# Adaptive products shared by three engines, and PSUM banks of their own in a fp32 network of mixers and experts

## The chip, the core and the metric

The kernel runs on one core of a Trainium2 chip. The metric is the device time of one execution, in microseconds. A core has TensorE (PE, matrix products into PSUM), VectorE (DVE), ScalarE (ACT), GpSimd (POOL) and SyncE (SP, which here only issues DMA transfers). Each engine has a queue of its own and works through it in order; they meet at semaphores.

## What is computed

All in fp32, for one sequence of 256 tokens of width 1024. A first network of two layers, each a mixer and a convolutional feed-forward stage, then a second block (context, two recurrent mixers, neighbourhood attention, a mixture of experts). The part that matters here is the first network and the vectors that modulate it:

```python
c_act = jax.nn.silu(c)
for l in range(DEPTH):
    mod = (c_act @ ada_w[l] + ada_b[l])[:, None, :]
    sh1, sc1, g1, sh2, sc2, g2 = jnp.split(mod, 6, axis=-1)
    h = _rmsnorm(x, norm_mix_w[l]) * (1 + sc1) + sh1
    x = x + g1 * _mixer(h, ...)
    h = _rmsnorm(x, norm_ffn_w[l]) * (1 + sc2) + sh2
    x = x + g2 * _conv_ffn(h, ffn_w_up[l], ffn_conv_w[l], ffn_conv_b[l], ffn_w_down[l])
```

`c` has batch 1, so `c_act @ ada_w` is a product of a vector with a 1024 x 6144 matrix for each layer; the second block has such a matrix too, used for its context and for its latents. In the mixer, queries and keys come from low-rank latents (`c_q` of 384, `c_kv` of 256, each normed and multiplied by an up-projection), beside them a gated recurrence whose gates are 16 columns of the same input projection:

```python
c_q, c_kv, k_rope, q_m, k_m, v_m, o_m, i_m, f_m, g_mla, g_mlstm = jnp.split(h @ w_in, ...)
q  = _rmsnorm(c_q, q_norm_w) @ w_uq ; kv = _rmsnorm(c_kv, kv_norm_w) @ w_ukv
merged = sigmoid(g_mla) * (y_mla @ w_br_mla) + sigmoid(g_mlstm) * (y_mlstm @ w_br_mlstm)
return merged @ w_out
```

## The kernel before

Activations lie transposed, 128 features on the partitions and 256 tokens along the row. A weight comes from memory in loads of 1 MB (`load`, L442, a tile `raw` of 128x2048; three such buffers, four in the context part at the start), in a fixed order on SP's queue. `split_w` turns each half of 128x1024 into a high part (`hi`, a cast on ACT, L451) and the rest (`lo`, raw - hi on DVE, L453); an activation is split in the same way into `hhi` and `hlo`. One fp32 product is then three matmuls, L474 (high x high), L475 (activation's low) and L476 (weight's low), for each block of 128x128.

PSUM has eight banks, handed out by tag: two `d`, three `a`, two `y`, one `f`. A tile of a tag waits until the tile that had the bank before has been read.

The modulating vectors are computed without PE. `ada` (L524) loads 1 MB, that is two blocks of 128x1024 in which each row belongs to one output, and DVE multiplies each block by the broadcast `c` and sums along the row, in one instruction (L533, `accum_out`). There are 80 such loads: 8 at the start, for the context's own vector, 8 behind the context part, then 64 in the two layers. All but the first 8 are a background generator: `tick()` is called at fixed places of the foreground code and adds a rate to each generator's account; a generator that has a whole step advances by one load. `ADA_PARTS` says which eight columns of the vectors (four loads) belong to which of the four stages, `ADA_RATE` how fast they go; `drain` does what is left at a stage's end.

The foreground in one layer: `mixer` (L660) computes the latents: `latent` squares them on ACT (L684) and scales them by the norm's weight (L685), `normed` forms the reciprocal root and the split `lat`. The third query latent is the first half of a `y` bank (`p2`), and its second half takes the rotated key part and the gates. Then the keys (`keys`, from two `d` banks, read by ACT L718 and DVE L719), the rotated key part (`krm`, a product with `rep`, L731), the values (`pv`, L487 to L489, in two `d` banks), the queries, a convolution, attention and recurrence. The branch projections come last: of each group of four output blocks, two `d` and two `y` banks are merged by the gates (L957 to L959: `mga`, `mgb`) and split into `hhi` and `hlo` for the output projection `wo`. `ffn` (L987) then norms `x`, and alternates up and down products; POOL's only steady work there is `hidl`, the low half of a hidden row (L459, 128x256).

The program's order on each engine is not the order of the code: a scheduler that sees priorities, estimated costs and free buffers sets it, except for the loads.

Of the kernel before, what the change touches and what calls it, by code (L numbers as in the profile page):

```python
# [15 lines left out]
AF = mybir.ActivationFunctionType  # L16
OP = mybir.AluOpType
# [3 lines left out]
T = 256  # L21
# [11 lines left out]
NA_PARTS = {3: (0, "wo2b"), 5: (4, "wo2e"), 7: (6, None)}  # L33
ORDER = ('load',)

ADA_PARTS = (range(2, 6), range(6, 9), range(9, 14), range(14, 18))
ADA_RATE, RK_RATE, MID_RATES = (0.8, 0.45, 0.95, 0.6), 0.8, (0.6, 1.0, 1.0, 1.0, 0.6)

# [311 lines left out]
class Net:  # L352
# [162 lines left out]
    def silu_row(self, c, eng=None):  # L515
# [5 lines left out]
        nc.vector.scalar_tensor_tensor(t, th, 1.0, t, OP.add, OP.mult)  # L521
        return t

    def ada(self, src, c, bias, mod, parts, pool=None):  # L524

        nc = self.nc
        for s in parts:
            for q in range(4 * s, 4 * s + 4):
                raw = self.load(src[q], pool, 3 if pool is None else CX_RAW)
                for r in range(2):  # L530
                    j = 2 * q + r
                    w = raw[:, r * 1024 : r * 1024 + 1024]
                    nc.vector.scalar_tensor_tensor(w, w, 0.5, c, OP.mult, OP.mult, accum_out=mod[:, j : j + 1])  # L533
                yield
            m = slice(8 * s, 8 * s + 8)
            nc.vector.tensor_tensor(mod[:, m], mod[:, m], bias[:, m], OP.add)
# [123 lines left out]
    def mixer(self, l, mp, x, mod):  # L660
        nc = self.nc
        s = str(l)
        mt = lambda shape, name, dt=F32, tag=None: mp.tile([P] + shape, dt, tag=tag or name, name=self.uid(name))
        v2 = lambda ap: ap.rearrange("p (a t) -> p a t", a=2)
        h = self.norm_mod(x, self.V("nmix" + s, 0, 8), mod[:, 8:16], mod[:, 0:8])
# [9 lines left out]
        st = Stream(self, "lat" + s)  # L675
        lat = mt([16, T], "lat", F32R)
        cq, ckv = (tuple(lat[:, o + i * n : o + i * n + n, :] for i in (0, 1)) for o, n in ((0, 3), (6, 2)))
        raw = mt([8, T], "raw", F32, "qf")
# [4 lines left out]
        def latent(j, ps, w):  # L683
            nc.scalar.activation(sqk[:, j, :], ps, AF.Square)  # L684
            nc.scalar.activation(raw[:, j, :], ps, AF.Identity, scale=w)  # L685
# [16 lines left out]
            latent(3 + q, pkv[:, q * T : q * T + T], self.V("kvn" + s, q))  # L702
        for q in range(2):
            latent(q, p01[:, q * T : q * T + T], self.V("qn" + s, q))
        p2 = self.ps("y")
        self.mm3(p2[:, :T], st, h)
        normed(ckv, 3, 2, 256)
        latent(2, p2[:, :T], self.V("qn" + s, 2))
        self.mm3(p2[:, T:], st, h)


        cqp, ckvp = self.parts(cq, range(3)), self.parts(ckv, range(2))
# [1 line left out]
        st = Stream(self, "uq" + s)  # L714

        def keys(b):
            pq = v2(self.proj(st, ckvp))
            nc.scalar.copy(kf[0:64, 4 * b : 4 * b + 4 : 2, :], pq[0:64])  # L718
            nc.vector.tensor_copy(kf[0:64, 4 * b + 1 : 4 * b + 4 : 2, :], pq[64:128])  # L719
# [2 lines left out]
        normed(cq, 0, 3, 384, False)  # L722

        krm = mt([T], "krm")
        nc.vector.tensor_tensor(krm[64:128, :], p2[64:128, T:], self.cs[64:128, :], OP.mult)
        gi, gf = self.tmp(T, "gi", bufs=1, rows=8), self.tmp(T, "gf", bufs=1, rows=8)
        nc.vector.tensor_scalar(gi, p2[0:8, T:], self.V("gb" + s)[0:8], None, OP.add)
        nc.vector.tensor_scalar(gf, p2[32:40, T:], self.V("gb" + s)[32:40], None, OP.add)
        keys(1)
        pk = self.ps("a")  # L730
        nc.tensor.matmul(pk[:, :T], self.C("rep")[64:128, :], krm[64:128, :], start=True, stop=True)  # L731
        nc.scalar.copy(kf[64:128], bcn(pk[64:128, :T], 8))
        pv = [self.ps("d") for _ in range(2)]
        self.mm3n(pv, st, ckvp, 512, False)
        for i in range(2):
            nc.scalar.copy(vn[:, i, :], pv[i])
# [106 lines left out]
        for hd in range(8):  # L843
# [10 lines left out]
            for i, c in enumerate((slice(0, P), slice(P, 3 * P))):  # L854
                nc.scalar.activation(e[:, c], ps[:, c], AF.Exp, bias=mx[:, i : i + 1], scale=(64 + 32) ** -0.5,
                                     accum_out=msum[:, i, hd : hd + 1])
# [89 lines left out]
        st = Stream(self, "br" + s)  # L946
        fl = lambda ap: ap.rearrange("p a t -> p (a t)")
        for j0 in (0, 4):
            pas, pbs = ([self.ps(t) for _ in range(2)] for t in "dy")
            for ps, yp in ((pas, yap), (pbs, ymp)):  # L950
                for q in range(4):
                    self.mm3(ps[q // 2][:, q % 2 * T : q % 2 * T + T], st, yp)
                    if q % 2 and ps is pbs:
                        j = j0 + q - 1
                        pa, pb = pas[q // 2], pbs[q // 2]
                        ta, tb = self.tmp(512, "mga"), self.tmp(512, "mgb")
                        nc.vector.scalar_tensor_tensor(ta, fl(sg[:, j : j + 2, :]), 1.0, pa, OP.add, OP.mult)  # L957
                        nc.vector.scalar_tensor_tensor(tb, fl(sg[:, 8 + j : 10 + j, :]), 1.0, pb, OP.add, OP.mult)
                        nc.vector.tensor_tensor(ta, ta, tb, OP.add)  # L959
                        self.split(m[0][:, j : j + 2, :], m[1][:, j : j + 2, :], v2(ta))  # L960
                        self.tick()
        gh = self.np.tile([P, 8], F32, tag="gh", name=self.uid("gh"))
        nc.vector.tensor_scalar(gh, mod[:, 16:24], 0.5, None, OP.mult)
        st = Stream(self, "wo" + s)
        mp_ = self.parts(m, range(8))
        for i in range(4):
            ps = self.proj(st, mp_)
            for c in range(2):
                j = 2 * i + c
# [17 lines left out]
    def ffn(self, l, fp, x, mod, rk):  # L987
# [14 lines left out]
        self.background(rk, RK_RATE)  # L1002
        self.background(self.ada_of(ADA_PARTS[2 * l + 1]), ADA_RATE[2 * l + 1])
        for op in _ffn_order():
# [77 lines left out]
    def first(self):  # L1082
        nc, x = self.nc, self.x
        with self.pool("cxm") as cxp, self.pool("cb") as self.cbp:
            with self.pool("rope") as rp:
# [7 lines left out]
                for l in range(2):  # L1093
                    self.part = 1
                    self.background(self.ada_of(ADA_PARTS[2 * l]), ADA_RATE[2 * l])
                    with self.pool(f"mix{l}") as mp, self.phase(f"m{l}", {256: 6, 384: 5, 512: 5}):
# [1072 lines left out]
```

## Time and profile before

| | us |
|---|---|
| runs: median of 3 (lowest to highest) | 1775.16 (1772.66 to 1775.33) |
| the profiled execution, its own time | 1772.79 |
| its span, first to last instruction | 1770.9 |
| mean granted clock of TensorE, share of full speed | 0.946 |
| busy: PE / DVE / ACT / POOL | 1579.1 / 1128.0 / 758.6 / 77.9 |

By the trace the context part runs to about 128 us, the first mixer to 310, its feed-forward stage to 550, the second mixer to 765, its feed-forward stage to 1003, the second block's mixers to 1314, and the experts to the end. A row of a timeline reads: start, duration, engine, line, operation, output tile <- input tiles, shape, and in brackets how long the engine was idle before it and what it waited for. A row of waits reads: who waited for whom, us in total, times, longest. Matmuls overlap: a row shows 0.28 us where one follows the other about every 0.12 us. The names of tiles are those of the code; where a line belongs to a helper (L442, L451, L453, L458, L459, L474 to L476), the tile tells what it is.

### The profile page before, as it was taken

The page shows a single profiled execution, that of the slowest core. Times are in us where ns is not written, and L with a number is a line of the kernel's source. Part 1 is how long each engine was busy: PE and PEld are TensorE (multiplying, and loading weights), DVE is VectorE, ACT ScalarE, POOL GpSimd, SP SyncE. Part 2 cuts the span into 40 slices and gives each one's busy share as a digit, 9 for nine tenths or more (in the row PEclk, how much of TensorE's full clock was granted, in tenths as well). Part 3 has the DMA queues.
Part 4 walks back from the last instruction along what each step waited for, and adds up shares of the span by engine and source line. Part 5 has one row for each costly group of instructions (what it writes and reads, how often), then busy time and mean ns, then how long its engine had stood idle before and what let it go on. Part 6 is the DMA issues. An engine that isn't in the chain of part 4 may idle for free.

```text
span 1770.9 us, 32054 instructions
## 1 busy us (share of the span) xinstructions
PE 1579.1 (89%) x13278; PEld 1269.7 (72%) x13278; DVE 1128.0 (64%) x2167; ACT 758.6 (43%) x1256; POOL 77.9 (4%) x81
## 2 busy tenths in 40 slices
PE   3989999999998999989999999999989877776766
PEld 2988999899998899979999999878874312221211
DVE  7979878798887898879989778766662111011011
ACT  3566545664455654556454576464431100000000
POOL 0000000020010000001010101000000000000000
PEclk7999999999999999999999999998989889888888
DMA  9745675556674478565667543123369999999998
GB/s 392 312 142 191 242 281 204 209 207 221 217 250 143 169 266 319 216 237 179 239 228 289 194 171 114 67 98 134 144 249 403 419 417 416 417 416 419 419 417 340
DMA packets 76808, 460.78 MB, mean 260 GB/s; under 512 B 8563, under 2 KB 11123, under 8 KB 28147
## 3 DMA queue, kind: packets, MB, share of 16 engines
q1 hardware_dynamic: 74352, 452.45, 67.0%
q10 hardware_dynamic: 2306, 6.24, 1.0%
q8 instruction: 106, 1.74, 0.4%
q14 instruction: 44, 0.35, 0.1%
HBM read 457.61 MB, written 1.05 MB: 259 GB/s over the span
## 4 chain that ended last, share of the span: by engine, by line
PE 63%; DMA 23%; DVE 8%; ACT 4%; issue 2%; POOL 0%; SPq 0%; DVEq 0%; ACTq 0%; POOLq 0%
DMA ew<-in_wgu 11%; PE d L474 10%; PE d L476 10%; PE d L475 10%; DMA ew<-in_wdown 8%; PE y L474 4%; PE y L476 3%; PE y L475 3%; PE a L1392 3%; DVE lo L453 2%; PE d L2052 2%; DVE raw L533 2%; PE a L1981 1%; PE a L628 1%; DMA raw<-in_ws 1%
## 5 line engine op out<-in xcount | busy, mean ns | idle before, releaser
L451 ACT CAST hi<-raw 128x1024 fp32r<-128x1024 f32 x309 | 322.4, 1048 | 303.2 <-PE d L475 186.2
L453 DVE TENSOR_TENSOR lo<-raw,hi 128x1024 fp32r<-128x1024 f32 x309 | 379.1, 1233 | 90.3 <-ACT hi L451 88.5
L474 PE MATMUL d<-hhi,hi 128*128 128x256 f32 x1320 | 387.9, 295 | 29.4 <-ACT hhi L591 23.7
L475 PE MATMUL d<-hlo,hi 128*128 128x256 f32 x1320 | 381.3, 289 | 3.2 <-DVE hlo L594 1.7
L476 PE MATMUL d<-hhi,lo 128*128 128x256 f32 x1320 | 380.2, 288 | 0.2 <-DVE lo L453 0.2
L474 PEld LDWEIGHTS d<-hhi,hi 128*128 128x128 f32 x1320 | 258.4, 196 | 38.3 <-ACT hhi L591 26.3
L475 PEld LDWEIGHTS d<-hlo,hi 128*128 128x128 f32 x1320 | 259.3, 196 | 6.6 <-DVE hlo L594 2.9
L476 PEld LDWEIGHTS d<-hhi,lo 128*128 128x128 f32 x1320 | 259.0, 196 | 1.4 <-DVE lo L453 0.4
L2052 PE MATMUL d<-ew,xe 128*32 128x512 f32 x984 | 165.3, 704 | 56.5 <-DMA ew<-in_wgu 56.0
L533 DVE SCALAR_TENSOR_TENSOR raw<-raw,cb 128x1024 f32<-128x1024 f32 x160 | 193.9, 1228 | 5.4 <-DMA raw<-in_ada 5.0
L2052 PEld LDWEIGHTS d<-ew,xe 128*32 128x32 f32 x984 | 26.1, 116 | 170.5 <-DMA ew<-in_wgu 145.7
L2057 DVE SCALAR_TENSOR_TENSOR moa<-moa,d 128x512 f32<-128x512 f32 x8 | 5.5, 687 | 178.4 <-ACT moa L2056 178.4
L474 PE MATMUL y<-hhi,hi 128*128 128x256 f32 x352 | 100.8, 286 | 4.6 <-ACT raw L685 3.9
L476 PE MATMUL y<-hhi,lo 128*128 128x256 f32 x352 | 100.0, 285 | 0.9 <-DVE lo L453 0.9
L475 PE MATMUL y<-hlo,hi 128*128 128x256 f32 x352 | 99.6, 283 | 0.0
L2070 PE MATMUL y<-ew,mht 128*32 128x512 f32 x472 | 74.4, 687 | 26.6 <-DMA ew<-in_wdown 22.4
L2088 DVE SCALAR_TENSOR_TENSOR x<-f,mod_l,x 128x256 f32<-128x256 f32 x32 | 14.0, 479 | 127.8 <-PE f L2084 127.8
L459 POOL TENSOR_TENSOR hidl<-fgel,hidh 128x256 fp32r<-128x256 f32 x44 | 54.2, 1233 | 838.4 <-ACT hidh L458 817.3
L2056 ACT ACTIVATE moa<-d 128x512 f32<-128x512 f32 x8 | 4.8, 597 | 184.7 <-PE d L2052 184.7
L474 PEld LDWEIGHTS y<-hhi,hi 128*128 128x128 f32 x352 | 67.4, 192 | 6.1 <-ACT raw L685 4.7
L2070 PEld LDWEIGHTS y<-ew,mht 128*32 128x32 f32 x472 | 13.0, 117 | 78.3 <-DMA ew<-in_wdown 58.6
L476 PEld LDWEIGHTS y<-hhi,lo 128*128 128x128 f32 x352 | 67.4, 192 | 1.4 <-DVE lo L453 1.1
(676 smaller groups left out, 3193.7 us busy)
## 6 DMA issues: line engine op xcount, KB each, us to landing
raw<-in_ws SPq DMA_DIRECT2D x151, 1024.0 KB, 4.8
ew<-in_wgu SPq DMA_DIRECT2D x100, 1024.0 KB, 18.0
raw<-in_ada SPq DMA_DIRECT2D x80, 1024.0 KB, 4.9
ew<-in_wdown SPq DMA_DIRECT2D x46, 1024.0 KB, 19.7
ew<-in_wgu SPq DMA_DIRECT2D x46, 512.0 KB, 13.8
ew<-in_wdown SPq DMA_DIRECT2D x28, 512.0 KB, 12.5
two<-in_wgu SPq DMA_DIRECT2D x20, 256.0 KB, 8.4
two<-in_wdown SPq DMA_DIRECT2D x16, 256.0 KB, 8.1
```

Source lines behind the costliest of these rows:

```text
L451: f.append(nc.scalar.copy(hi_, raw))
L453: f.append(nc.vector.tensor_tensor(lo_, raw, hi_.bitcast(F32), OP.subtract))
L459: (eng or self.nc.vector).tensor_tensor(lo, src, hi.bitcast(F32), OP.subtract)
L474: nc.tensor.matmul(out, whi, hhi, start=first and i == 0, stop=False, **s)
L475: nc.tensor.matmul(out, whi, hlo, start=False, stop=False, **s)
L476: nc.tensor.matmul(out, wlo, hhi, start=False, stop=last and i == n - 1, **s)
L533: nc.vector.scalar_tensor_tensor(w, w, 0.5, c, OP.mult, OP.mult, accum_out=mod[:, j : j + 1])
L628: self.nc.tensor.transpose(out, in_, self.C("ident")[:k, :k])
L1392: nc.tensor.matmul(ps[r, g * 64 : g * 64 + 64], l_(g, p, r), r_(g, p, r), start=True, stop=True, skip_group_check=True)
L1981: nc.tensor.matmul(ps[:, k * P : k * P + P], xn[:, i, d : d + P], of(i), start=i == 0, stop=i == 1, skip_group_check=True)
L2052: nc.tensor.matmul(ps[32 * e : 32 * e + 32, :], xe[:, k, 32 * e : 32 * e + 32], w[e], start=k == 0, stop=k == 7, skip_group_check=True)
L2070: nc.tensor.matmul(py[q][32 * e : 32 * e + 32, :], ht[:, f * P + 32 * e : f * P + 32 * e + 32], w[e], start=f == 0, stop=f == 3, skip_grou ...
```

## The change

Three things, and two tables of numbers. First, the two blocks of each adaptive load are no longer treated alike: the first is multiplied by POOL in place and then halved and summed along its row by ACT; the second stays on DVE. 80 of the 160 products of DVE become 80 of POOL and 80 of ACT. Second, the `tick()` after each of the four merges of the branch projections is gone; four loads (one range of `ADA_PARTS`) go from the second mixer's stage to the first feed-forward stage, and two rates are lower. Third, the third query latent and the gates have a `y` bank each (`p2`, `pg`), and the values take two `y` banks where they took two `d` banks.

```diff
-ADA_PARTS = (range(2, 6), range(6, 9), range(9, 14), range(14, 18))
-ADA_RATE, RK_RATE, MID_RATES = (0.8, 0.45, 0.95, 0.6), 0.8, (0.6, 1.0, 1.0, 1.0, 0.6)
+ADA_PARTS = (range(2, 6), range(6, 10), range(10, 14), range(14, 18))
+ADA_RATE, RK_RATE, MID_RATES = (0.8, 0.45, 0.8, 0.45), 0.8, (0.6, 1.0, 1.0, 1.0, 0.6)
...
+    def ada_block(self, w, c, out, shared):
+
+        nc = self.nc
+        if shared:
+            nc.gpsimd.tensor_tensor(w, w, c, OP.mult)
+            nc.scalar.activation(w, w, AF.Copy, scale=0.5, accum_out=out)
+        else:
+            nc.vector.scalar_tensor_tensor(w, w, 0.5, c, OP.mult, OP.mult, accum_out=out)
+
...
                 for r in range(2):
-                    j = 2 * q + r
-                    w = raw[:, r * 1024 : r * 1024 + 1024]
-                    nc.vector.scalar_tensor_tensor(w, w, 0.5, c, OP.mult, OP.mult, accum_out=mod[:, j : j + 1])
+                    self.ada_block(raw[:, r * 1024 : r * 1024 + 1024], c, mod[:, 2 * q + r : 2 * q + r + 1], r == 0)
                 yield
...
-        p2 = self.ps("y")
-        self.mm3(p2[:, :T], st, h)
+        p2, pg = (self.ps("y")[:, :T] for _ in range(2))
+        self.mm3(p2, st, h)
         normed(ckv, 3, 2, 256)
-        latent(2, p2[:, :T], self.V("qn" + s, 2))
-        self.mm3(p2[:, T:], st, h)
+        latent(2, p2, self.V("qn" + s, 2))
+        self.mm3(pg, st, h)
...
-        pv = [self.ps("d") for _ in range(2)]
+        pv = [self.ps("y") for _ in range(2)]
         self.mm3n(pv, st, ckvp, 512, False)
...
                         self.split(m[0][:, j : j + 2, :], m[1][:, j : j + 2, :], v2(ta))
-                        self.tick()
```

The order of the instructions moves at three places. The numbers behind a tile's name are the program's own and differ between the two kernels; lines after the new function are six or seven higher.

ACT near 41 to 55 us, in the context part; `x` (here `two_120..123<-x_74`, its four squares) has been loaded by then, `cpad` is the context's first projection, copied out of a `d` bank that PE needs again. Before:

```order
L451 CAST hi_37_281<-raw_36_279 128x1024
L451 CAST hi_39_309<-raw_36_279 128x1024
L451 CAST hi_44_350<-raw_43_348 128x1024
L561 ACTIVATE two_120_987<-x_74 128x512
L561 ACTIVATE two_121_989<-x_74 128x512
L561 ACTIVATE two_122_992<-x_74 128x512
L561 ACTIVATE two_123_997<-x_74 128x512
L451 CAST hi_46_378<-raw_43_348 128x1024
L541 ACT_TABLE_LOAD
L1216 COPY cpad0_222<-d_32_225 128x2x256
L1216 COPY cpad1_223<-d_33_226 128x2x256
```

Now:

```order
L451 CAST hi_37_289<-raw_36_287 128x1024
L451 CAST hi_39_317<-raw_36_287 128x1024
L529 ACTIVATE raw_41_351,mod0_75<-raw_41_351 128x1024
L451 CAST hi_44_359<-raw_43_357 128x1024
L529 ACTIVATE raw_48_418,mod0_75<-raw_48_418 128x1024
L451 CAST hi_46_387<-raw_43_357 128x1024
L568 ACTIVATE two_120_1003<-x_74 128x512
L568 ACTIVATE two_121_1005<-x_74 128x512
L1222 COPY cpad0_230<-d_32_233 128x2x256
L568 ACTIVATE two_122_1008<-x_74 128x512
L1222 COPY cpad1_231<-d_33_234 128x2x256
```

Two halves of adaptive blocks stand among the casts, and the first copy stands behind two squares where it stood behind four and a table load.

PE where the keys end and the values begin, layer 0 (`d_156`, `d_164` before and `d_157`, `d_165` now are the two banks of keys, `a_` the rotated key part, `d_166` before and `y_167` now the first bank of values). Before:

```order
L475 MATMUL d_164_1277<-lat_131_1039,hi_158_1244 128x256
L476 MATMUL d_164_1277<-lat_131_1039,lo_159_1245 128x256
L731 MATMUL a_165_1292<-krm_161_1271,kon_31_220 128x256
L487 MATMUL d_166_1295<-hi_168_1297,lat_131_1039 128x512
L488 MATMUL d_166_1295<-lo_169_1298,lat_131_1039 128x512
L489 MATMUL d_166_1295<-hi_168_1297,lat_131_1039 128x512
```

Now:

```order
L476 MATMUL y_148_1186<-hhi_125_1021,lo_154_1229 128x256
L699 MATMUL f_134_1058<-sqk_133_1057,ones_68 128x256
L474 MATMUL d_157_1258<-lat_131_1055,hi_159_1261 128x256
L474 MATMUL d_165_1294<-lat_131_1055,hi_159_1261 128x256
L738 MATMUL a_166_1309<-krm_162_1288,kon_31_228 128x256
L487 MATMUL y_167_1312<-hi_169_1314,lat_131_1055 128x512
L475 MATMUL d_157_1258<-lat_131_1055,hi_159_1261 128x256
L476 MATMUL d_157_1258<-lat_131_1055,lo_160_1262 128x256
```

The first matmul of each key bank, the rotated part and the first matmul of the values now come right behind the gates (`y_148`), before the rest of the keys.

ACT where the branch projections of layer 0 end and `wo` begins (`hhi_416` before and `hhi_417` now are the merged rows' high halves; the last of the four opens the last blocks of `wo`). Before:

```order
L451 CAST hi_462_3234<-raw_459_3204 128x1024
L458 CAST hhi_416_2919<-mga_450_3155 128x512
L451 CAST hi_466_3268<-raw_465_3266 128x1024
L458 CAST hhi_416_2919<-mga_455_3194 128x512
L382 DMA kon_482_3459<-in_k_rk 128x1216
```

Now:

```order
L451 CAST hi_458_3224<-raw_457_3222 128x1024
L529 ACTIVATE raw_462_3282,mod0_75<-raw_462_3282 128x1024
L451 CAST hi_460_3252<-raw_457_3222 128x1024
L458 CAST hhi_417_2949<-mga_449_3177 128x512
L451 CAST hi_465_3290<-raw_464_3288 128x1024
L529 ACTIVATE raw_469_3348,mod0_75<-raw_469_3348 128x1024
L458 CAST hhi_417_2949<-mga_453_3212 128x512
```

Two adaptive halves stand here, one of them just ahead of the last merged row's cast.

## Rows read from the trace of the kernel before

**Rows 1.** busy us (share of the span) of each engine, part 1 of the page

```profile
PE 1579.1 (89%) x13278; PEld 1269.7 (72%) x13278; DVE 1128.0 (64%) x2167; ACT 758.6 (43%) x1256; POOL 77.9 (4%) x81
```

**Rows 2.** busy time by stretches of the span; the first row names the columns

```profile
core 0: us, PE busy (x) PEld busy (x) DVE busy (x) ACT busy (x) POOL busy (x), PEclk, DMA share, GB/s
177.00:232.00 55.00, 52.83 (x429) 50.06 (x429) 48.63 (x89) 30.45 (x68) 0.00 (x0) 1.00 0.68 250
298.00:310.00 12.00, 12.00 (x103) 12.00 (x103) 11.86 (x18) 5.63 (x7) 0.00 (x0) 1.00 0.77 277
340.00:550.00 210.00, 208.39 (x2092) 202.46 (x2091) 181.67 (x313) 113.00 (x178) 27.45 (x22) 0.99 0.61 219
1314.00:1771.00 457.00, 344.23 (x2016) 113.78 (x2016) 63.98 (x173) 39.40 (x82) 0.38 (x1) 0.86 0.98 402
```

**Rows 3.** waits of PE, 340 to 550 us: us in total, times, longest us

```profile
PE y L475 <- POOL hidl L459: 1.4, 2, 1.0
```

**Rows 4.** costliest groups, part 5: busy us, mean ns of one | idle before

```profile
L451 ACT CAST hi<-raw 128x1024 fp32r<-128x1024 f32 x309 | 322.4, 1048 | 303.2 <-PE d L475 186.2
L453 DVE TENSOR_TENSOR lo<-raw,hi 128x1024 fp32r<-128x1024 f32 x309 | 379.1, 1233 | 90.3 <-ACT hi L451 88.5
...
L533 DVE SCALAR_TENSOR_TENSOR raw<-raw,cb 128x1024 f32<-128x1024 f32 x160 | 193.9, 1228 | 5.4 <-DMA raw<-in_ada 5.0
...
L459 POOL TENSOR_TENSOR hidl<-fgel,hidh 128x256 fp32r<-128x256 f32 x44 | 54.2, 1233 | 838.4 <-ACT hidh L458 817.3
```

**Rows 5.** single lines: times, duration in ns min/median/max, first and last start

```profile
L459 POOL TENSOR_TENSOR hidl<-fgel,hidh x44: 726/1298/1825, 360.5 to 1008.3; 128x256 fp32r<-128x256 f32 x44
...
L1728 POOL TENSOR_TENSOR two<-two,kon x8: 994/999/1108, 1183.3 to 1283.4; 128x384 f32<-128x384 f32 x8
...
L855 ACT ACTIVATION_READ_ACCUMULATOR esm<-a,mx x32: 192/197/206, 160.3 to 666.0; 128x1 f32 x32
```

**Rows 6.** timeline, 364 to 368 us: start us, us, engine, line, operation, tiles

```profile
364.51 2.90 DVE L453 TENSOR_TENSOR lo<-raw,hi 128x1024 fp32r<-128x1024 f32 x2
...
364.71 1.61 POOL L459 TENSOR_TENSOR hidl<-fgel,hidh 128x256 fp32r<-128x256 f32 x1 [2.68 <-ACT hidh L458]
```

**Rows 7.** timeline of the start, DVE and ACT, and a wait of PE

```profile
16.27 1.22 DVE L533 SCALAR_TENSOR_TENSOR raw<-raw,cb 128x1024 f32<-128x1024 f32 x1 [3.20 <-DMA raw<-in_ada]
...
18.75 1.22 DVE L533 SCALAR_TENSOR_TENSOR raw<-raw,cb 128x1024 f32<-128x1024 f32 x1
...
27.29 2.36 DVE L453 TENSOR_TENSOR lo<-raw,hi 128x1024 fp32r<-128x1024 f32 x2 [1.19 <-ACT hi L451]
...
36.87 0.43 ACTq L1183 DMA_DIRECT2D x<-in_xT  x1
...
48.99 2.20 ACT L561 ACTIVATE two<-x 128x512 f32<-128x512 f32 x4 [1.51 <-DMA x<-in_xT]
...
53.44 1.08 ACT L1216 COPY cpad<-d 128x512 f32<-128x512 f32 x2
...
PE d L474 <- ACT cpad L1216: 1.9, 1, 1.9
```

**Rows 8.** timeline of the latents, keys and values, layer 0

```profile
134.47 0.38 PE L474 MATMUL y<-hhi,hi 128*128 128x256 f32 x1 [1.92 <-ACT raw L685]
...
135.84 0.69 DVE L459 TENSOR_TENSOR lat<-raw,lat 128x512 fp32r<-128x512 f32 x1 [0.35 <-ACT lat L458]
...
143.17 0.94 DVE L459 TENSOR_TENSOR lat<-raw,lat 128x768 fp32r<-128x768 f32 x1
...
144.77 0.50 PE L487 MATMUL d<-hi,lat 128*128 128x512 f32 x1 [1.67 <-DVE kf L719]
```

**Rows 9.** waits of PE in the branch projections, layer 0, 284 to 298 us

```profile
PE d L474 <- ACT hi L451: 1.7, 2, 1.2
PE d L476 <- DVE lo L453: 0.2, 1, 0.2
```

**Rows 10.** timeline of DVE at the start of the output projection, layer 0

```profile
313.07 0.69 DVE L459 TENSOR_TENSOR hlo<-mga,hhi 128x512 fp32r<-128x512 f32 x1 [0.69 <-ACT hhi L458]
```

More of the change, by code (lines that the diff above doesn't have):

```diff
@@ L724, in mixer @@
         krm = mt([T], "krm")
-        nc.vector.tensor_tensor(krm[64:128, :], p2[64:128, T:], self.cs[64:128, :], OP.mult)
+        nc.vector.tensor_tensor(krm[64:128, :], pg[64:128], self.cs[64:128, :], OP.mult)
         gi, gf = self.tmp(T, "gi", bufs=1, rows=8), self.tmp(T, "gf", bufs=1, rows=8)
-        nc.vector.tensor_scalar(gi, p2[0:8, T:], self.V("gb" + s)[0:8], None, OP.add)
-        nc.vector.tensor_scalar(gf, p2[32:40, T:], self.V("gb" + s)[32:40], None, OP.add)
+        nc.vector.tensor_scalar(gi, pg[0:8], self.V("gb" + s)[0:8], None, OP.add)
+        nc.vector.tensor_scalar(gf, pg[32:40], self.V("gb" + s)[32:40], None, OP.add)
         keys(1)
```

## The prediction

> **What bounds the kernel now.** I read the busy table first, then the stages, then waits inside a stage. TensorE (PE) is busy 89% of the span, VectorE (DVE) 64%, ScalarE (ACT) 43%, GpSimd (POOL) 4% [rows 1]. By stretches [rows 2] the end of the program is another matter: from 1314 us on the DMA engines are busy 0.98 of the time and PE works on what they bring; no adaptive product and no mixer lies there, so what the change wins or loses before 1003 us is carried through as it is. In the stages that it touches, PE is busy 92 to 99% and hardly waits: in the 210 us of the first feed-forward stage its listed waits are 1.4 us [rows 3]. DVE, at 48.63 of 55 us in the attention [rows 2], is the next limit. So 105 us of DVE work taken away (80 products of 1.23 and an accumulator read of 0.08 us) is no 105 us of time: in most places PE has nothing to get back.
>
> **Price of a shared product.** Before, each 128x1024 block costs DVE 1.228 us, 160 in all [rows 4], and the read of the accumulator. The change sends 80 of them through POOL and ACT. No row shows POOL at 128x1024. Its 128x256 product takes 726 ns at best and its 128x384 one 994 ns [rows 5]: 268 ns for 128 more elements, so 726 + 768 x 2.09 = 2.33 us is my estimate. ACT then reads the block back: its pass over 128x1024 is 1.048 us [rows 4], and the accumulator read beside its exponentials is 0.197 us [rows 5], so 1.25 us. A block thus turns from 1.31 us of one engine into 3.6 us on two in a row.
>
> **POOL and DVE do not run side by side.** POOL's 128x256 product has a median of 1.298 us against 0.726 us at best [rows 5]. At 364.71 us it takes 1.61 us while two DVE differences with both inputs in SBUF, 2 x 1.22 us elsewhere, take 2.90 us around it [rows 6]: 0.88 us longer for POOL, some 0.5 us longer for DVE. One waits for the other. The Trainium skill has a rule against this change, "SBUF — State Buffer", section "Who interferes with whom": the port pair that POOL shares with DVE is locked for a whole instruction, and a DVE instruction with two SBUF inputs contends with a POOL instruction that reads SBUF; the stretched pair of rows agrees, and by the rule the sum is the forecast, without it the first rival.
>
> So I charge DVE for a held lock. It is in operations with two SBUF inputs most of the time (the casts' differences and the products alone are 573 of its 1128 us [rows 1, 4]); it runs into a 2.33 us hold somewhere between not at all and wholly. I take the middle, 1.2 us, because the differences come in pairs right behind the casts, and because POOL's hold is three times that of the row in which DVE lost 0.5. Saved 1.31, lost 1.2: DVE gains about nothing per block (bounds: it gains 1.31, or loses 1.02).
>
> **Start (0 to 58 us), 8 shared blocks.** Here DVE is a chain: products at the pace at which the loads land (16.27, 18.75: 2.48 us apart), two differences, four products, then the gain, h, and behind h's high half in ACT's queue the load of x at 36.87, which has landed 12.1 us later; the four squares of x start at 48.99, cpad at 53.44, and PE waits for cpad [rows 7]. A load would take 2.33 + 1.22 = 3.55 us where it took 2.45 with both blocks on DVE. Four loads lag by 4.4 us, DVE's idle 1.19 us before the differences [rows 7] absorbs a part, and the last two loads add 2.2: mod_c comes 5.4 us later, x lands near 54.3. ACT's new order gives back: cpad0 stands behind two squares and no table load, 1.1 us after x and not 4.45. So cpad at 55.4: +2.0, and with the two products of ACT in the same queue I take **+2.5** (bounds -1.5, were the lock nothing, and +6.5). The 8 blocks of the context's background: **+1** (0 to +3, at 0.4 us each).
>
> **Latents and values in their own banks.** The gate product waited 1.92 us for ACT to read the latents out of the same bank, and the values 1.67 us for DVE to empty a d bank [rows 8]; both waits have lost their cause, once in each of the two layers. The second goes whole, since in the new order the first value product is far ahead of its rest and the query latents, 143.17 + 0.94 = 144.1, are in time. Of the first, what is late next is the low half of the key latents, ready at 135.84 + 0.69 = 136.5 [rows 8]; the gate product used to end near 137.4, so 0.9 is left. Two layers: 2 x 2.6 = **-5.1** (bounds -7.2 and -2).
>
> **No tick beside the branch projections.** PE loses 1.7 us there to a cast and 0.2 to a difference, layer 1 alike [rows 9]: the weight loads stood in the 3 raw buffers behind adaptive ones, and DVE had products between the merges. Two layers: **-3.8** (bounds -5 and 0). But the steps that left are now at the branch's end and in the output projection: one load's ACT product stands just before the last hhi, whose difference DVE waited for at 313.07 already [rows 10], and its POOL product has to be over first. PE has the first seven blocks of the projection to cover it, 21 products of 0.117 us (103 in 12 us, [rows 2]) = 2.5 us, against 2.33 + 0.5 + 1.25 = 4.1 us of POOL and ACT behind the landing. I take **+2.5** for both layers together (0 to +6).
>
> **Attention** (13 shared blocks in each layer): DVE stays as full as it was, and ACT, whose exponentials and casts PE works on next, gets 13 x 1.25 = 16 us more. Between nothing and 0.4 us per block, 0 to 5 us; I take 2 per layer, **+4**. **Norms before the feed-forward stages**: one POOL product lands among the sixteen two-input operations by which h is made: between 0 and 2.3 a layer, **+1.5**. **Feed-forward**: 32 shared blocks; PE's waits of 1.4 us show the cover, and ACT has 113 of 210 us in use [rows 2]. The first stage also takes four loads from the second mixer. **+2** (-2 to +8).
>
> Sum: 2.5 + 1 - 5.1 - 3.8 + 2.5 + 4 + 1.5 + 2 = +4.6 us. The profiled execution took 1772.79 us (span 1770.9), 2.4 below the median of 1775.16; so 1777.4 for it, and **1780** against the median. A difference of 0.2%, 3.5 us, is about what a measurement of this kernel can tell from no change.
>
> **Rivals.** (A) *The lock hardly costs DVE anything*: POOL slips between, starts as soon as a load lands (its queue is nearly empty in these stages), and DVE keeps its 1.31 us per block. Then the start costs nothing (2.33 us per load is under the landing pace of 2.48), norms and feed-forward nothing, attention wins about 2 where PE waits for DVE. For it: the shortest POOL products show no wait at all [rows 5], and DVE is idle a third of the span [rows 1]. Against: the median of 1.298. It gives -5.1 - 3.8 - 2 = -10.9: 1764. (B) *ACT waits in its queue for POOL*, on the slow side: in the new order ACT's half stands about eight PE products, 1 us, behind POOL's, which needs 2.33 + 0.5 with the mean wait of the page (1.233 - 0.726); so ACT stalls some 1.8 us each time with casts behind it, whose differences wait behind them on DVE, and PE behind both. If 0.35 us of that comes through for each of the 72 blocks after the start: 25 - 8.9 + 3.5 = +20: 1795. It decides from about 0.2 us a block. For it: DVE already waits 88.5 us for casts [rows 4]. Against: PE's cover in the feed-forward stages, and loads that often land before their turn. (C) *The banks and ticks do not give what they say*: what stands next is just as late, and sharing is neutral: 1775.
>
> **How the numbers follow.** The forecast 0.47 (faster 0.03, same 0.15, slower 0.29); A 0.30, all faster; B 0.16, all slower; C 0.07 (0.01, 0.05, 0.01). Faster 0.34, same 0.20, slower 0.46. Alone, the forecast runs from 1773 to 1787. The range takes in A at 1764 and B at 1795 and a little beyond: 1763 to 1797.
>
> **What would show it.** POOL's product near 2.3 us at its least and near 2.9 at its median; DVE differences and products of 2 us and over beside it, so that DVE's busy time falls by far less than 105 us (under A it falls by about 100). cpad near 55.4 and PE's first long row after it 2 us later. No wait of PE at the gate product beyond 1 us, none at the values, none for casts in the branch. The forecast is wrong if the span to 1003 us shrinks (A), or if PE's waits for casts in the feed-forward stages come to over 10 us (B); it is also wrong in its steps if the mixer keeps its length while the start does not grow.

## The result and the profile after

The changed kernel takes 1847.97 us (median of 4 runs, 1842.55 to 1860.35) against 1774.13 us: a ratio of 1.0426, 95% interval 1.0373 to 1.0479, **74 us slower**. The side was the one forecast, the size was not: 1780 had been given and 1797 was the end of the range.

The profiled execution of the changed kernel took 1860.35 us, the slowest of the four, 12 us above their median, so its trace shows a loss of 88 us where the runs say 74. Its busy times and costliest groups (parts 1 and 5 of the page; us in total, mean ns of one, then the idle time before):

```profile
PE 1606.2 (86%) x13278; PEld 1292.9 (70%) x13278; DVE 1161.7 (63%) x2013; ACT 831.3 (45%) x1408; POOL 302.1 (16%) x161
...
L453 DVE TENSOR_TENSOR lo<-raw,hi 128x1024 fp32r<-128x1024 f32 x309 | 421.0, 1369 | 101.3 <-ACT hi L451 99.7
...
L528 POOL TENSOR_TENSOR raw<-raw,cb 128x1024 f32<-128x1024 f32 x80 | 227.6, 2849 | 604.9 <-DMA raw<-in_ada 346.7
...
L529 ACT ACTIVATE raw<-raw 128x1024 f32<-128x1024 f32 x80 | 84.8, 1060 | 164.1 <-POOL raw L528 163.8
L531 DVE SCALAR_TENSOR_TENSOR raw<-raw,cb 128x1024 f32<-128x1024 f32 x80 | 128.8, 1613 | 36.4 <-DMA raw<-in_ada 36.1
```

Against [rows 1] and [rows 4]: DVE does 80 instructions fewer that took 1.31 us each, and is busy 34 us longer. The differences that stayed on it went from 1233 to 1369 ns each, its 80 remaining products from 1228 to 1613 ns. ACT stood 163.8 us before its halves, waiting for POOL. The shortest, median and longest of POOL's product, by its line:

```profile
L528 POOL TENSOR_TENSOR raw<-raw,cb x80: 2328/2684/3467, 12.8 to 1084.3; 128x1024 f32<-128x1024 f32 x80
```

The stages (busy us of each engine, then the granted clock, DMA share, GB/s): attention of layer 0, and the two feed-forward stages.

```profile
core 0: us, PE busy (x) PEld busy (x) DVE busy (x) ACT busy (x) POOL busy (x), PEclk, DMA share, GB/s
195.00:255.00 60.00, 53.25 (x408) 50.51 (x408) 45.63 (x73) 34.18 (x71) 17.39 (x6) 0.94 0.64 228
356.00:605.00 249.00, 225.99 (x2158) 216.59 (x2157) 208.92 (x321) 137.90 (x224) 70.44 (x38) 0.96 0.57 208
868.00:1106.00 238.00, 220.65 (x2125) 213.31 (x2124) 197.56 (x313) 127.28 (x204) 69.96 (x37) 0.95 0.60 216
```

PE used to be busy 208.39 of 210 us in such a stage at a granted clock of 0.99 [rows 2]; now it is 226 of 249 at 0.96. The matmuls are the same 13278; at half clock each of them is busy for longer (step 4 below).

Where the time came from is read by the casts of the weights' halves (L451): there are 309 in each kernel, in the same order, so the start of the same cast tells how far a kernel has come. The third column is a kernel of the experiments, the changed kernel with all products on DVE; its distance to the changed kernel is what the sharing cost in each stretch. These are single executions: that of the changed kernel is 12 us above the median of its runs, that with all on DVE 9.

| stretch, from cast to cast | changed - before, us | all on DVE - before | sharing costs | its terms in the prediction |
|---|---|---|---|---|
| start and context (to 24) | +11.4 | -0.2 | 11.6 | 3.5 |
| mixer 0 (to 72) | +10.4 | -4.3 | 14.7 | 3.2 |
| feed-forward 0 (to 144) | +30.5 | +4.4 | 26.0 | 1.8 |
| mixer 1 (to 198) | +8.8 | -6.8 | 15.5 | 3.2 |
| feed-forward 1 (to 270) | +25.9 | -1.1 | 27.0 | 1.8 |
| behind them (to 288) | 0.0 | +1.5 | -1.4 | 0 |
| sum | +87.0 | -6.5 | 93.4 | 13.5 |

More than half of the cost, 53 of 93 us, lies in the two stages that the prediction held to be covered. The other parts of the change do gain what was forecast of them.

### The profile page after: what moved, and what is told of

It reads as the page before. It is cut to its first block, busy times and chain, and to the rows that moved or that the text cites. A ratio compares the mean times of both kernels' runs of the same rounds, so it can differ in the third digit from the quotient of the medians.

```text
span 1858.5 us, 32319 instructions
## 1 busy us (share of the span) xinstructions
PE 1606.2 (86%) x13278; PEld 1292.9 (70%) x13278; DVE 1161.7 (63%) x2013; ACT 831.3 (45%) x1408; POOL 302.1 (16%) x161
## 5 line engine op out<-in xcount | busy, mean ns | idle before, releaser
L453 DVE TENSOR_TENSOR lo<-raw,hi 128x1024 fp32r<-128x1024 f32 x309 | 421.0, 1369 | 101.3 <-ACT hi L451 99.7
L451 ACT CAST hi<-raw 128x1024 fp32r<-128x1024 f32 x309 | 321.0, 1046 | 204.8 <-PE d L475 125.0
L476 PE MATMUL d<-hhi,lo 128*128 128x256 f32 x1320 | 384.5, 292 | 5.8 <-DVE lo L453 5.7
L528 POOL TENSOR_TENSOR raw<-raw,cb 128x1024 f32<-128x1024 f32 x80 | 227.6, 2849 | 604.9 <-DMA raw<-in_ada 346.7
L529 ACT ACTIVATE raw<-raw 128x1024 f32<-128x1024 f32 x80 | 84.8, 1060 | 164.1 <-POOL raw L528 163.8
L531 DVE SCALAR_TENSOR_TENSOR raw<-raw,cb 128x1024 f32<-128x1024 f32 x80 | 128.8, 1613 | 36.4 <-DMA raw<-in_ada 36.1
L2076 PE MATMUL y<-ew,mht 128*32 128x512 f32 x472 | 69.8, 654 | 28.3 <-DMA ew<-in_wdown 24.2
```

Of the source, the lines that this page charges most:

```text
L451: f.append(nc.scalar.copy(hi_, raw))
L453: f.append(nc.vector.tensor_tensor(lo_, raw, hi_.bitcast(F32), OP.subtract))
L476: nc.tensor.matmul(out, wlo, hhi, start=False, stop=last and i == n - 1, **s)
L528: nc.gpsimd.tensor_tensor(w, w, c, OP.mult)
L529: nc.scalar.activation(w, w, AF.Copy, scale=0.5, accum_out=out)
L2076: nc.tensor.matmul(py[q][32 * e : 32 * e + 32, :], ht[:, f * P + 32 * e : f * P + 32 * e + 32], w[e], start=f == 0, stop=f == 3, skip_grou ...
```

## Experiments

Two theories stood at the start. Theory 1: POOL's product, reading SBUF, keeps DVE out, and PE runs out of rows behind DVE. Theory 2: ACT, whose half stands soon behind POOL's in its queue, waits for POOL with casts behind it. A third came out of the runs: POOL holds the load's buffer longer, so that the next load is issued late. A ratio is that of a kernel to the kernel before measured on the same chip; 1% is 17.7 us. The experiments ran on several chips, so what one costs over another is taken from their ratios and not from their medians. Where POOL's product is left out or comes too late, the vectors are wrong; apart from one kernel, told below, PE still does the same 13278 matmuls, and the times can be compared.

**All 160 products on DVE** (the other parts of the change stay).

```diff
-self.ada_block(raw[...], c, mod[...], r == 0)
+self.ada_block(raw[...], c, mod[...], False)
```

> The changed kernel with all 160 products on DVE again; the PSUM banks, the tables and the missing ticks of the branch stay. Both theories (DVE shut out by POOL's reads; ACT's queue held up by POOL) say the whole loss of 74 us goes, and what is left is the gain of the other parts: 1774 - 5.1 - 3.8 = 1765 us. If the tables or the moved steps cost something by themselves, 1774 or more.

Measured: 1762.03 us, ratio 0.9942 (0.9918 to 0.9966), 10 us faster than before. So the sharing alone carries the loss: 0.9942 to 1.0426 is 4.84%, 86 us, 1.07 us for each of the 80 blocks.

**The sharing alone**, put into the kernel before.

> The kernel before with the sharing alone (80 products to POOL and ACT; old banks, ticks and tables). Both theories: slower than the changed kernel by what its other parts gain, 1848 + 9 = 1857 us. If the other parts interact badly with the sharing (the rates crowd the feed-forward stage), below 1840.

Measured: 1858.13 us, ratio 1.0502 (1.0458 to 1.0547). The sharing costs 89 us without the other parts and 86 with them: within the uncertainty (about 0.5% each) the parts add up, and the tables of rates have no visible share in the loss.

**POOL only writes** the block, twice, and ACT waits for that as before.

```diff
-            nc.gpsimd.tensor_tensor(w, w, c, OP.mult)
+            for _ in range(2): nc.gpsimd.memset(w, 0.0)
```

> The changed kernel with POOL filling the block twice with zeros in place of the product: about 2 us of POOL per block that reads nothing, and ACT waits for it as before. The product itself is left out, so the vectors are wrong by half. Theory 1 (POOL's read shuts DVE out): DVE's differences and products go back to 1.23 us and the time to 1780 us or below. Theory 2 (ACT stands in its queue until POOL is done): most of the loss stays, 1830 us or more, with ACT waiting over 100 us for POOL.

Measured: 5699.56 us, which is no comparison: with these vectors the experts get more work (PE does 27278 matmuls and not 13278), and the last part takes over 4 ms. Up to the experts the trace can be compared: cast 288 starts at 1065.5 us, 12 us earlier than before and 5.5 earlier than with all on DVE, one execution of each. POOL's fills, the differences of DVE and ACT's wait (groups by line, then a row of the waits):

```profile
L528 POOL MEMSET raw<- 128x1024 f32 x160 | 152.6, 954 | 575.6 <-DMA raw<-in_ada 346.6 <-DVE lo L453 108.3 <-issue 72.3
```

```profile
L453 DVE TENSOR_TENSOR lo<-raw,hi 128x1024 fp32r<-128x1024 f32 x309 | 376.6, 1222 | 125.2 <-ACT hi L451 121.8
```

```profile
ACT raw L529 <- POOL raw L528: 52.7, 40, 3.5
```

POOL works 1.9 us on each block right in front of ACT, DVE's differences are at 1222 ns, and nothing is lost. This is against theory 2 as the main cause, and it agrees with the rule of the Trainium skill named in the prediction ("SBUF — State Buffer", "Who interferes with whom"), in its other half: a POOL instruction that only writes SBUF does not contend with a DVE instruction of two inputs.

**ACT first, POOL afterwards.** Nobody waits for POOL's result.

```diff
-            nc.gpsimd.tensor_tensor(w, w, c, OP.mult)
             nc.scalar.activation(w, w, AF.Copy, scale=0.5, accum_out=out)
+            nc.gpsimd.tensor_tensor(w, w, c, OP.mult)
```

> The changed kernel with the two halves of a shared block swapped: ACT sums the unmultiplied block as soon as it is there, POOL multiplies it afterwards and nobody reads its result, so the vectors are wrong. DVE is shut out as before, ACT waits for nothing of POOL. Theory 1: 1835 us or more, DVE's operations as long as in the changed kernel. Theory 2: 1785 us or below.

Measured: 1834.96 us, ratio 1.0365 (1.0327 to 1.0403). ACT's wait for POOL is gone and 0.61% is won, 11 us with an uncertainty of about as much (the two intervals together give 0.65%). Theory 2 is at most a small part; the rest stays, and DVE's operations are longer than ever. Its busy times (part 1), then its two groups on DVE:

```profile
PE 1594.9 (87%) x13278; PEld 1284.2 (70%) x13278; DVE 1176.3 (64%) x2019; ACT 831.0 (45%) x1402; POOL 299.2 (16%) x161
```

```profile
L453 DVE TENSOR_TENSOR lo<-raw,hi 128x1024 fp32r<-128x1024 f32 x309 | 434.3, 1412 | 77.4 <-ACT hi L451 75.8
L531 DVE SCALAR_TENSOR_TENSOR raw<-raw,cb 128x1024 f32<-128x1024 f32 x80 | 129.8, 1625 | 38.5 <-DMA raw<-in_ada 38.3
```

**The same without POOL's product.**

> The kernel e4 (ACT's half first, nobody waits for POOL) without POOL's product: 80 blocks are summed by ACT unmultiplied, and POOL does nothing for them. The vectors come out as in e4, wrong in the same way. Theory 1 (POOL's read shuts DVE out): DVE has 105 us less to do and nobody blocks it: 1750 to 1762 us, some 75 us below e4. If ACT's own load were the cost: within 20 us of e4.

Measured: 1750.05 us, ratio 0.9895 (0.9860 to 0.9931). The same vectors as in the kernel just told, the same work on ACT; only POOL's product is missing, and 4.70% with it, **83 us**.

```profile
PE 1573.8 (90%) x13278; PEld 1265.9 (73%) x13278; DVE 1043.1 (60%) x2017; ACT 831.5 (48%) x1404; POOL 77.0 (4%) x81
```

```profile
L453 DVE TENSOR_TENSOR lo<-raw,hi 128x1024 fp32r<-128x1024 f32 x309 | 376.9, 1224 | 134.7 <-ACT hi L451 132.2
L531 DVE SCALAR_TENSOR_TENSOR raw<-raw,cb 128x1024 f32<-128x1024 f32 x80 | 97.4, 1219 | 17.9 <-DMA raw<-in_ada 17.6
```

DVE is busy 133 us less: that is what POOL's 80 products took from it, 1.66 us each. PE's listed waits, summed over the first 1160 us, fall from 117.5 to 57.6 us; those for the weights' low halves, which DVE forms, with the product and without:

```profile
PE d L476 <- DVE lo L453: 14.1, 8, 2.8
```

```profile
PE d L476 <- DVE lo L453: 0.5, 2, 0.2
```

This is theory 1. The kernel also shows how little there was to win: with 80 products off DVE and nothing on POOL in their place it is only 0.47% faster than with all on DVE, 8 us with an uncertainty of as much.

**Half as many shared blocks**, every other load.

```diff
-self.ada_block(raw[...], c, mod[...], r == 0)
+self.ada_block(raw[...], c, mod[...], r == 0 and q % 2 == 0)
```

> The changed kernel with 40 of the 160 products shared in place of 80 (every other load). If each shared block costs the same wherever it lies: half of the way from 1762 to 1848, 1805 us. If the cost comes from crowding (two POOL products close together, ACT's queue filling up), nearer to 1785.

Measured: 1802.54 us, ratio 1.0170 (1.0126 to 1.0213): 2.28% above all-on-DVE for 40 blocks, 1.01 us each, where 80 cost 1.07 each. The cost goes with the number; crowding has no visible share.

**Shared in the feed-forward stages alone** (`r == 0 and self.part == 2`).

> The changed kernel with the sharing in the two feed-forward stages alone (32 products; the 48 others on DVE). By the prediction these stages hide nearly all of it: 1762 + 2 = 1764 us. By the cost per block that the half-shared kernel showed (1.0 us a block anywhere): 1762 + 32 = 1794 us; by the changed kernel's trace, in which the two stages alone grew by some 45 us: 1805 us.

Measured: 1804.88 us, ratio 1.0155 (1.0107 to 1.0203): 2.13%, 38 us for 32 blocks, 1.2 us each, give or take 0.3. The stages that were to hide the blocks pay about as much for one as the others, or more.

**The banks alone, and the ticks with the tables alone** (the kernel before with only that part).

> The kernel before with the PSUM banks alone (p2 and pg in two y banks, the values in y). By the prediction's term: -5.1 us, so 1768.5 against 1773.5. If the next wait is just as late: no change.

> The kernel before without the ticks beside the branch projections and with the new tables, nothing shared. By the prediction's term: -3.8 us at the branch, a little given back where the output projection starts: 1770 to 1772. If what moved costs as much where it now stands: no change.

Measured: ratio 0.9992 (0.9967 to 1.0016) and 0.9980 (0.9958 to 1.0003). Both intervals take in the expected gain (-0.3%, -0.2%) and also no change: undecided one by one. Together, in the kernel with all on DVE, they are 0.9942.

**POOL's product in four pieces**, as the changed kernel waits for it, and with ACT first.

```diff
-            nc.gpsimd.tensor_tensor(w, w, c, OP.mult)
+            for k in range(0, 1024, 256): nc.gpsimd.tensor_tensor(w[:, k : k + 256], w[:, k : k + 256], c[:, k : k + 256], OP.mult)
```

> The changed kernel with POOL's product cut into four of 128x256, so that DVE can get in after 0.73 us and not after 2.33; POOL works 4 x 0.73 = 2.9 us on a block. If the length of one hold is what hurts (DVE stands for a whole instruction, PE runs out of rows): 1815 us or below. If the sum of the holds counts (DVE loses what POOL takes): 1848 us or above.

> The kernel e4 (ACT's half first, nobody waits for POOL, vectors wrong as there) with POOL's product in four pieces of 128x256. It tells apart the two readings of the kernel with four pieces, in which DVE's operations were hardly longer and ACT waited 282 us for POOL. If its 1937 us came from ACT's queue waiting for a product four times interrupted: well below e4's 1835, about 1790, since DVE loses less to a short hold. If DVE's loss to POOL counts however it is cut: 1835 us or above.

Measured: 1936.58 us, ratio 1.0928 (1.0891 to 1.0966), and 1871.40 us, ratio 1.0535 (1.0502 to 1.0568). Both times lie where the second reading had put them, but not for its reason. Shorter holds do spare DVE: its differences are down to 1263 ns from 1369, and it is busy 67 us less than in the changed kernel; yet the kernel is 89 us slower. With ACT waiting, the rows of the first are these (busy times; DVE's differences; ACT's wait):

```profile
PE 1631.2 (85%) x13278; PEld 1312.4 (68%) x13278; DVE 1094.9 (57%) x2013; ACT 827.2 (43%) x1408; POOL 417.8 (22%) x401
```

```profile
L453 DVE TENSOR_TENSOR lo<-raw,hi 128x1024 fp32r<-128x1024 f32 x309 | 388.4, 1263 | 163.7 <-ACT hi L451 161.9 <-PE a L635 0.7
```

```profile
ACT raw L529 <- POOL raw L528: 281.8, 63, 9.6
```

ACT's wait rises from 164 to 282 us: the product is done later, four pieces of 1.115 us in the mean where one took 2.849. Swapping the halves takes 70 us of it away (1.0928 to 1.0535), so here theory 2 is real. What is left is still 30 us above the uncut product with ACT first, and there the waits for loads have grown (ACT and DVE for their blocks of an adaptive load):

```profile
ACT raw L528 <- DMA raw<-in_ada: 131.5, 57, 7.8
DVE raw L531 <- DMA raw<-in_ada: 108.5, 48, 6.7
```

With one product ACT's was 60.2 us and DVE's 38.3. That agrees with the third theory, of a buffer that POOL holds longer.

**A product that belongs to nothing.** ACT sums as in the kernel without a product; POOL then multiplies columns of `c` by themselves into a tile of its own, holding no load. (`spare` is a tile of 128x944 in bf16; its first column is copied from ACT's sum, so that the product starts behind it.)

```diff
+            nc.gpsimd.tensor_copy(self.spare[:, :1], out)
+            nc.gpsimd.tensor_tensor(self.spare, c[:, :944], c[:, :944], OP.mult)
```

> The kernel e5 (ACT sums the unmultiplied block, vectors wrong as there) with a product on POOL that belongs to nothing: after each of ACT's 80 sums POOL multiplies 944 columns of the broadcast c by themselves into a tile of its own. It holds no buffer of a load and nobody waits for its result, so what is left of e4 is POOL's reading beside DVE. If DVE's loss to POOL's reads is the cause: 944/1024 of the way from 1750 to 1835, 1820 us or more. If it was the load's buffer, held until POOL is done: 1765 us or below.

Measured: 1805.23 us, ratio 1.0175 (1.0156 to 1.0193), 2.80% or 50 us above the kernel without it, between the two readings. Its busy times, and the spare product:

```profile
PE 1589.6 (88%) x13278; PEld 1279.8 (71%) x13278; DVE 1113.7 (62%) x2017; ACT 832.3 (46%) x1404; POOL 284.8 (16%) x241
```

```profile
L530 POOL TENSOR_TENSOR spare<-cb x80: 1758/1761/2842, 19.7 to 1025.0; 128x944 bf16<-128x944 f32 x80
```

With a result of 2 bytes an element and one tile as both inputs the product takes 1.76 us and not 944/1024 of 2.33, which the expectation had reckoned with. It holds no load, so these 50 us are POOL's reading beside DVE, but for one thing: at the start DVE's addition to `mod_c`, which overwrites what the one-column copy reads, waits for that copy, 8.0 us in two waits.

**Two spare products of 624 columns**, as much reading as the real product.

> The kernel e12 with two spare products of 624 columns in place of one of 944 (vectors wrong as there), about 2 x 1.17 us of POOL per block, as much reading as in e4's one product of 2.33 us, and again no buffer of a load held. If POOL's reading beside DVE is all of e4's loss: 1835 us. If a third of it was the load's buffer, held until POOL is done: 1815 to 1825 us. If a longer hold costs no more than e12's: 1805 us.

Measured: 1813.76 us, ratio 1.0200 (1.0176 to 1.0225): 3.05%, **54 us** above the kernel without.

```profile
L530 POOL TENSOR_TENSOR spare<-cb x160: 1217/1229/2313, 20.9 to 1039.6; 128x624 bf16<-128x624 f32 x160
```

At 2 x 1.23 us of reading per block, a little more than the real product's, it comes out next to the figure expected for a third in the buffer. The wait for the copy is here as well, and larger:

```profile
DVE mod_c L544 <- POOL spare L529: 14.9, 2, 9.3
```

The gain comes at 46.26 us, against 40.71 in the kernel with ACT first and 32.89 in that without the product, so the start is no clean comparison. Behind it, from cast 24 to cast 288, the traces are 43.3 us (spare products) and 65.5 us (product on the load) longer than without a product. By the ratios it is 54 of 83 us, each with an uncertainty of about 8. Both ways about two thirds of what POOL's product costs when nobody waits for it are its reading, and a third comes with its standing on the load itself. For that third two things are seen. The issue of the next load waits for POOL as the last to leave the buffer, which it never does in the kernels with spare products; in the kernel with ACT first:

```profile
SPq L442 <- POOL raw L529: 146.2, 56, 9.3
```

And DVE's products, on the other block of the same load, take 1625 ns there against 1340 beside the two spare products. How the third divides between the two was not told apart.

The ladder, each step one thing more, by the ratios: no POOL (0.9895), its reading (1.0200), the reading on the load (1.0365), ACT waiting for it (1.0426). The last step is as small as its uncertainty.

## Why the prediction was wrong

**What was right.** POOL's product, put at 2.33 us from two shorter rows, is 2.328 at its least; ACT's half, put at 1.25, is 1.060 and 0.186 for the read. The other parts were put at -8.9 us, and the kernel with all on DVE is 10 us faster (interval 6 to 15); in its trace the two mixers gain 4.3 and 6.8 us, and the first feed-forward stage, which took over four loads, loses 4.4. The first gate wait did turn into one for the latents' low half, put at 1.0 us (1.92 less 0.9), and the wait before the values is gone; PE's row of the first in the changed kernel:

```profile
PE d L475 <- DVE lat L459: 1.0, 1, 1.0
```

**Step 1, the hold, mis-sized.** DVE was charged 1.2 us per block. Busy times give (1161.7 - 1128.0 + 80 x 1.31) / 80 = **1.73 us**, near the 1.66 of the experiment. The middle of the bounds was taken, with the argument that DVE runs into a hold somewhere. In the mean it loses 1.7 us of a product that takes 2.85; an operation with two SBUF inputs stands until POOL is done, whatever its size. POOL in the first feed-forward stage, and DVE beside it:

```profile
422.94 2.38 POOL L528 TENSOR_TENSOR raw<-raw,cb 128x1024 f32<-128x1024 f32 x1
...
423.49 0.48 DVE L1024 SCALAR_TENSOR_TENSOR facc<-y,vec,facc 128x255 f32<-128x255 f32 x1
423.88 0.70 DVE L1414 STREAM_TRANSPOSE at<-kt 128x512 f32<-128x512 f32 x1
424.51 0.44 DVE L1024 SCALAR_TENSOR_TENSOR facc<-y,vec,facc 128x254 f32<-128x254 f32 x1
424.87 1.54 DVE L531 SCALAR_TENSOR_TENSOR raw<-raw,cb 128x1024 f32<-128x1024 f32 x1
```

POOL holds from 422.94 to 425.32. The two facc operations with an input in PSUM (0.48, 0.44) and the transposition with one input (0.70) run at their usual length; the product with two inputs, begun at 424.87 with 0.45 us of the hold to go, takes 1.54 us and not 1.22. This block cost DVE only 0.3 us; the one at 909.62 us, under step 3, cost it 1.75. At the start of the program there is no such cover, and even an addition of 8 columns waits: POOL, then DVE.

```profile
12.79 15.87 POOL L528 TENSOR_TENSOR raw<-raw,cb 128x1024 f32<-128x1024 f32 x6 [12.36 <-DVE gw L620]
30.51 5.93 POOL L528 TENSOR_TENSOR raw<-raw,cb 128x1024 f32<-128x1024 f32 x2 [1.85 <-DMA raw<-in_ada]
44.07 5.07 POOL L528 TENSOR_TENSOR raw<-raw,cb 128x1024 f32<-128x1024 f32 x2 [7.62 <-DVE cb L521]
```

```profile
26.32 2.37 DVE L543 TENSOR_TENSOR mod_c<-mod_c,vec 128x8 f32<-128x8 f32 x1 [4.49 <-ACT raw L529]
...
30.89 6.63 DVE L453 TENSOR_TENSOR lo<-raw,hi 128x1024 fp32r<-128x1024 f32 x2
...
40.12 0.17 DVE L608 SCALAR_TENSOR_TENSOR gain<-mod_c,vec 128x8 f32<-128x8 f32 x1
...
43.91 6.70 DVE L601 SCALAR_TENSOR_TENSOR hlo<-two,mod_c,hhi 128x256 fp32r<-128x256 f32 x6
50.53 3.02 DVE L597 SCALAR_TENSOR_TENSOR two<-xc,gain,rstd 128x256 f32<-128x256 f32 x2
```

The addition to mod_c took 2.37 us where it takes 0.17, the pair of differences 6.63 where it took 2.36 [rows 7].

**Step 2, the start, with the right chain and a stop too early.** Start and context were put at 3.5 us and cost 11.6. The gain was put 5.4 us later and came 5.7 later (40.12 against 34.47 in the trace before); x was issued at 43.31 against 36.87. But the next two shared blocks, of the context's background, fell on the forming of the context's h, which the prediction put at 1 us for all eight, 0.4 each at most: six operations from 43.91 took 6.70 us, two more 3.02. ACT's queue behind them:

```profile
43.31 0.44 ACTq L1189 DMA_DIRECT2D x<-in_xT  x1
53.19 0.51 ACT L598 ACTIVATE hhi<-two,mod_c 128x256 fp32r<-128x256 f32 x1 [9.78 <-DVE two L597]
...
62.22 1.15 ACT L568 ACTIVATE two<-x 128x512 f32<-128x512 f32 x2
64.35 0.59 ACT L1222 COPY cpad<-d 128x512 f32<-128x512 f32 x1 [0.98 <-PE d L476]
```

The next high half of h waited 9.78 us for DVE, and cpad came at 64.35: 10.9 us later than [rows 7], not 2.0. PE had less cover here than the 92 to 99% that the prediction gives for the stages it touches: from 35 to 58 us it was busy 18.95 of 23 us in the trace before.

**Step 3, the cover in the feed-forward stages, the largest error.** "PE's waits of 1.4 us show the cover" was the step: +2 us, at most +8 (with 1.5 more for the norms), where the stages took 53. Few waits showed only that PE's rows had come in time from a DVE that was busy 181.67 of 210 us; they said nothing of a delay of 2.4 to 3 us in one piece. One such piece (POOL, DVE, two rows of ACT, PE):

```profile
908.92 2.59 POOL L528 TENSOR_TENSOR raw<-raw,cb 128x1024 f32<-128x1024 f32 x1 [0.69 <-DMA raw<-in_ada]
...
909.62 2.97 DVE L531 SCALAR_TENSOR_TENSOR raw<-raw,cb 128x1024 f32<-128x1024 f32 x1
...
911.54 1.06 ACT L529 ACTIVATE raw<-raw 128x1024 f32<-128x1024 f32 x1 [2.61 <-POOL raw L528]
...
913.04 0.57 ACT L1410 COPY y<-a 128x512 f32<-128x512 f32 x1
...
913.67 1.54 PE L1398 MATMUL a<-y,at 64*64 64x64 f32 x24 [4.94 <-ACT y L1410]
```

The load has landed, POOL and DVE start on its two blocks, DVE's takes 2.97 us. ACT waits 2.61 us for POOL; behind its half in the queue stands the copy of y, and PE, in whose queue the recurrence of the background stands among the rows of the stage, waits 4.94 us for that copy. The prediction named ACT's queue in rival B and put 0.2 us a block as the point from which it decides; measured is 1.07, from both engines together.

**Step 4, PE's clock, missing in the sum.** After this pause PE works on at half its clock. The stretches around that wait (columns as in the table of stages; the third number from the end is the granted clock):

```profile
910.00:912.00 2.00, 0.00 (x0) 0.00 (x0) 2.00 (x1) 0.46 (x1) 1.51 (x1) 1.00 0.80 254
912.00:914.00 2.00, 0.33 (x6) 0.33 (x8) 1.82 (x6) 2.00 (x5) 0.00 (x0) 0.72 1.07 336
914.00:916.00 2.00, 2.00 (x34) 1.88 (x31) 1.30 (x3) 1.64 (x4) 0.72 (x1) 0.50 0.77 315
916.00:918.00 2.00, 2.00 (x11) 2.00 (x11) 2.00 (x5) 0.00 (x0) 0.00 (x0) 0.50 0.38 152
918.00:920.00 2.00, 2.00 (x13) 2.00 (x12) 1.22 (x2) 0.40 (x1) 0.00 (x0) 0.57 0.00 0
920.00:922.00 2.00, 2.00 (x19) 2.00 (x18) 1.32 (x2) 0.95 (x2) 0.97 (x1) 1.00 0.00 0
```

PE stood still or nearly so from 910 to 913, and from 914 to 918 the granted clock is 0.50, the level of 1.2 GHz; by 920 it is back at 1.00. From 128 us to the end of the second feed-forward stage (cast 270), what the clock withheld (1 less the granted clock, summed over the time) is 11.9 us before, 10.2 with all on DVE and 41.0 in the changed kernel, in 5, 4 and 17 drops. PE was busy in 18.3 us of this half-clock time with all on DVE and in 71.7 us in the changed kernel. If it did half the work in them, (71.7 - 18.3) / 2 = some 27 of the 93.4 us by which these two traces differ are no waiting, but rows at half speed after a wait. This is an estimate, from an execution whose mean clock, 0.931, is the lowest of the changed kernel's four (the others 0.935 to 0.937). A pause has to be priced with what follows it; the trace of before had five such drops to learn from.

**The rivals.** A fell: DVE kept none of its saving. C fell. B had the place of one part, ACT's queue (164 us of waiting, 2.8 us a time where 1.8 was put), but taking this wait away won 11 us only, with an uncertainty of as much. The lock was in the forecast itself; it was taken for neutral.

## What to carry to other kernels

Work taken from a busy DVE and given to POOL is only taken away if POOL does not read SBUF while DVE has operations with two SBUF inputs to do: here 1.31 us saved per block cost 1.7 us of DVE, and 1.07 us of the kernel's time. Few waits on the bounding engine say that its supply comes in time, not that it would if each delay came in one piece of 2.5 us; compare the piece with how far ahead the supplier is, and add the stretch at half clock that follows a pause such as those here. Cutting the product into short pieces spares the neighbour a little and makes everyone who waits for the product later.

## What the runs showed that was not expected

That a hold does not depend on the size of what it holds up: 2.37 us for an addition of 8 columns that takes 0.17. That four pieces of 128x256 cost the kernel 89 us more than one of 128x1024, though a piece takes 0.712 us at its least and DVE is busy 67 us less. And that the clock took some 27 us, by the estimate under step 4, beside 64 us of longer waits: PE's listed waits, summed over the first 1160 us, are 133.8 us in the changed kernel and 69.4 with all on DVE.
